# Attention in units of four heads on a fixed clock of twelve matmuls, with engines held to program order

## The chip, the cores and the metric

The kernel runs on one core of one Trainium2 chip. The metric is the device time of one execution, in microseconds (us), as the median of three runs.

## The reference, cut to what matters

One sequence of 256 positions and width 1024 goes through two transformer blocks (the second with weights of its own form), and every product is a float32 product.

```python
def first_block(x, ...):                # DEPTH = 2, layer 0 even, layer 1 odd
    h = x
    for layer in range(DEPTH):
        hn = rmsnorm(h, mix_norm[layer])
        if layer % 2 == 0:
            h = h + moba_nsa_mixer(hn, ...)     # 8 MoBA heads + 8 NSA heads of 64
        else:
            h = h + fox_mixer(hn, ...)          # 16 heads, cumulative forget bias
        h = h + sqrelu_mlp(rmsnorm(h, mlp_norm[layer]), mlp_w1[layer], mlp_w2[layer])
    return rmsnorm(h, final_norm)

def second_block(x, c, ...):
    n = modulate(rmsnorm_2(h, g_ffn1), sh1, sc1);  h = h + 0.5 * gt1 * swiglu(n, ...)
    n = modulate(rmsnorm_2(h, g_mix), sh2, sc2);   h = h + gt2 * hybrid_mixer(n, ...)  # pooling + 8 heads
    n = modulate(rmsnorm_2(h, g_ffn2), sh3, sc3);  h = h + 0.5 * gt3 * swiglu(n, ...)
    return rmsnorm_2(h, g_final)

# in fox_mixer, per head and block of 128 queries:
cum = jnp.cumsum(log_f, axis=1)
s = einsum('bhqd,bhkd->bhqk', qc, k) * scale + cq[..., None] - cum[:, :, None, :]
p = masked_softmax(s, key_pos <= t);   o = einsum('bhqk,bhkd->bhqd', p, v)
```

## The kernel before, in words

**Weight products.** Activations stand transposed, features on partitions and 256 positions along the row. A product with a weight matrix is split in high and low halves (type fp32r) and made of three matmuls per tile (`mm3`, L331 to L333): high by high, high weight by low activation, low weight by high activation. 8304 such matmuls are issued, each 256 (or 258) columns wide. The weights come from HBM in raw tiles of up to 1 MB on SP's DMA queue. Each raw tile is converted in two halves of 128x1024: ACT copies it into a high half (`wh`, L237), DVE subtracts that from the raw tile into the low half (`wl`, L238). Five buffers of each hold the halves, so a half is converted while the four before it are used (`conv`, L219, and `Weights.half`, L251).

**The other work** is put between the weight matmuls. After every twelve weight matmuls the program calls `poke` (L298). It writes one conversion, then the steps of a norm whose countdown is over (`later`, `stage`), then one step of background work (`bg`, L281), where up to two generators are under way.

**Attention** is written as such generators. A `pair_unit` (L645) takes two heads of 64: the scores (QK, L650 and L651, one bank of PSUM per head), on DVE the bias and the row minimum (L660, L661), on ACT the exponentials (L662, L664), on DVE the division (L668 to L676), on PE three transposes per head (L681) with a copy by ACT (L683), and the product with the values (PV, L694 and L696). There are 24 such pairs: eight for NSA (two branches of four), four for MoBA, eight for forget attention (layer 1), four in the hybrid mixer. A third branch of NSA attends to compressed keys (`compress`, `cmp_unit`, L944 to L1053).

**The order of each engine's queue** is not the program's: a scheduler orders the instructions by their dependences and its own estimates. A PSUM bank is taken by tag (`bank(tag, 2)`, L82): four tags, `g`, `a`, `accA` and `accB`, with two banks each.

**Norms.** The squares are summed over the partitions by matmuls (L482), POOL takes the inverse root, and `spread` (L494) brings it to all partitions: ACT writes a diagonal (L497), two float32 matmuls with a matrix of ones broadcast it (L498), ACT copies it out (L500). At a stage's end `feed` (L473) splits the new activations into high (L423, ACT) and low (L424, DVE), which the next stage's first matmuls read.

**Forget attention** needs the running sum of the log gates in every partition. `forget` (L1097): two transposes on PE (L1111), a scan on DVE (L1114), one DMA to DRAM (`cd`, L1116) and four back (`hh<-cd`, 512 KB each, L1118), all issued by ACT, then per four heads one add of the causal mask on POOL (L1122), and per head one more (`pre`, L1149).

## Time and profile before

| | |
|---|---|
| median of 3 runs | 1129.63 us (1129.22 to 1130.44) |
| profiled execution, its own time | 1130.82 us |
| span of its trace | 1128.6 us |
| PE busy | 1107.9 us, 98% |
| DVE busy | 806.9 us, 71% |
| ACT busy | 580.6 us, 51% |
| POOL busy | 95.1 us, 8% |
| DMA moved | 233.72 MB, 207 GB/s on average |

The time outside the span (2.2 us) lies before the first and after the last traced instruction. Matmuls overlap in the records: a weight matmul is listed with 0.28 us, yet the next one starts after less than half of that, so times on PE are read from start to start. A row with "x4" joins four records of one line that follow one another; a float32 matmul leaves two records.

### The profile page before, as it was taken

The page shows a single profiled execution, that of the slowest core. Times are in us where ns is not written, and L with a number is a line of the kernel's source. Part 1 is how long each engine was busy: PE and PEld are TensorE (multiplying, and loading weights), DVE is VectorE, ACT ScalarE, POOL GpSimd, SP SyncE. Part 2 cuts the span into 40 slices and gives each one's busy share as a digit, 9 for nine tenths or more (in the row PEclk, how much of TensorE's full clock was granted, in tenths as well). Part 3 has the DMA queues.
Part 4 walks back from the last instruction along what each step waited for, and adds up shares of the span by engine and source line. Part 5 has one row for each costly group of instructions (what it writes and reads, how often), then busy time and mean ns, then how long its engine had stood idle before and what let it go on. Part 6 is the DMA issues. An engine that isn't in the chain of part 4 may idle for free.

```text
span 1128.6 us, 22520 instructions
## 1 busy us (share of the span) xinstructions
PE 1107.9 (98%) x9104; PEld 1070.4 (95%) x9104; DVE 806.9 (71%) x1547; ACT 580.6 (51%) x975; POOL 95.1 (8%) x135
## 2 busy tenths in 40 slices
PE   8999999999999999999999999999999999999997
PEld 7868899999999999999999999999999999999997
DVE  6657678887876665887878777756587867775654
ACT  5466556454546655654544655544455465444432
POOL 3000020000012400300000320000020010000001
PEclk9899999999999999999999999999999999999999
DMA  8954259999986643689998657565474546656521
GB/s 239 331 188 150 76 165 335 314 322 304 311 256 201 207 142 113 222 284 315 305 305 282 183 157 200 181 183 183 148 220 150 151 113 191 185 184 187 178 85 38
DMA packets 243720, 233.72 MB, mean 207 GB/s; under 512 B 6353, under 2 KB 227185, under 8 KB 243617
## 3 DMA queue, kind: packets, MB, share of 16 engines
q1 hardware_dynamic: 242272, 229.37, 64.8%
q10 hardware_dynamic: 1184, 2.73, 0.7%
q8 instruction: 71, 1.16, 0.4%
q14 instruction: 33, 0.26, 0.1%
q0 software_dynamic: 160, 0.19, 0.1%
HBM read 230.42 MB, written 1.85 MB: 206 GB/s over the span
## 4 chain that ended last, share of the span: by engine, by line
PE 89%; DVE 5%; ACT 3%; issue 1%; DMA 1%; SPq 0%; POOL 0%; POOLq 0%; ACTq 0%
PE g L331 10%; PE g L332 10%; PE g L333 10%; PE accA L332 6%; PE accA L331 6%; PE accA L333 6%; PE a L333 6%; PE a L331 6%; PE a L332 6%; PE accB L332 5%; PE accB L331 5%; PE accB L333 5%; DVE wl L238 2%; DVE nl L424 1%; PE a L651 1%; PE accA L681 1%
## 5 line engine op out<-in xcount | busy, mean ns | idle before, releaser
L238 DVE TENSOR_TENSOR wl<-raw,wh 128x1024 fp32r<-128x1024 f32 (+3 forms) x356 | 427.4, 1205 | 207.2 <-ACT wh L237 206.1
L237 ACT ACTIVATE wh<-raw 128x1024 fp32r<-128x1024 f32 (+3 forms) x356 | 365.8, 1033 | 367.3 <-PE accB L332 101.7
L331 PE MATMUL g<-nh,wh 128*128 128x256 f32 (+1 forms) x880 | 253.3, 288 | 0.3 <-DVE ev L1287 0.3
L332 PE MATMUL g<-nl,wh 128*128 128x256 f32 (+1 forms) x880 | 250.2, 284 | 3.3 <-DVE nl L424 3.3
L333 PE MATMUL g<-nh,wl 128*128 128x256 f32 (+1 forms) x880 | 249.9, 284 | 0.0
L331 PEld LDWEIGHTS g<-nh,wh 128*128 128x128 f32 x880 | 167.6, 190 | 6.7 <-issue 4.7
L332 PEld LDWEIGHTS g<-nl,wh 128*128 128x128 f32 x880 | 167.3, 190 | 5.2 <-DVE nl L424 5.0
L333 PEld LDWEIGHTS g<-nh,wl 128*128 128x128 f32 x880 | 167.3, 190 | 1.3 <-DVE wl L238 0.7
L333 PE MATMUL a<-nh,wl 128*128 128x258 f32 (+1 forms) x576 | 162.8, 283 | 0.0
L331 PE MATMUL a<-nh,wh 128*128 128x258 f32 (+1 forms) x576 | 162.3, 282 | 0.0
L332 PE MATMUL a<-nl,wh 128*128 128x258 f32 (+1 forms) x576 | 162.0, 281 | 0.0
L332 PE MATMUL accB<-hl,wh 128*128 128x256 f32 x432 | 123.1, 285 | 0.0
L332 PE MATMUL accA<-hl,wh 128*128 128x256 f32 x432 | 123.1, 285 | 0.0
L333 PE MATMUL accB<-hh,wl 128*128 128x256 f32 x432 | 120.8, 280 | 0.0
L333 PE MATMUL accA<-hh,wl 128*128 128x256 f32 x432 | 120.7, 279 | 0.0
L331 PE MATMUL accA<-hh,wh 128*128 128x256 f32 x432 | 120.4, 279 | 0.0
L331 PE MATMUL accB<-hh,wh 128*128 128x256 f32 x432 | 120.3, 279 | 0.0
L331 PEld LDWEIGHTS a<-nh,wh 128*128 128x128 f32 x576 | 109.0, 189 | 0.0
L332 PEld LDWEIGHTS a<-nl,wh 128*128 128x128 f32 x576 | 108.9, 189 | 0.0
L333 PEld LDWEIGHTS a<-nh,wl 128*128 128x128 f32 x576 | 108.7, 189 | 0.0
L408 DVE SCALAR_TENSOR_TENSOR ada<-ada,cb 128x1024 f32<-128x1024 f32 x72 | 87.7, 1219 | 16.1 <-DMA ada<-in_w_adaT_dram 15.7
L331 PEld LDWEIGHTS accA<-hh,wh 128*128 128x128 f32 x432 | 81.2, 188 | 0.0
(298 smaller groups left out, 1971.6 us busy)
## 6 DMA issues: line engine op xcount, KB each, us to landing
raw<-in_mlp_w_dram SPq DMA_DIRECT2D x64, 1024.0 KB, 7.2
ada<-in_w_adaT_dram SPq DMA_DIRECT2D x72, 512.0 KB, 5.9
raw<-in_w_gate_dram SPq DMA_DIRECT2D x44, 512.0 KB, 4.0
raw<-in_w_up_dram SPq DMA_DIRECT2D x44, 512.0 KB, 5.3
raw<-in_w_down_dram SPq DMA_DIRECT2D x16, 1024.0 KB, 5.2
raw<-in_odd_w_in_dram SPq DMA_DIRECT2D x11, 1024.0 KB, 5.7
raw<-in_even_w_in_dram SPq DMA_DIRECT2D x8, 1024.0 KB, 7.7
raw<-in_w_in_dram SPq DMA_DIRECT2D x8, 1024.0 KB, 5.7
```

The costliest lines, as they stand in the source:

```text
L237: state["conva"] = act.activation(his[u][:, k:k + m], r[:, k:k + m], AF.Copy).ins
L238: state["conv"] = dve.tensor_tensor(los[u][:, k:k + m], r[:, k:k + m], his[u][:, k:k + m].bitcast(F32), OP.subtract).ins
L331: pe.matmul(ps, wh, xh, start=start, stop=False, **kw)
L332: pe.matmul(ps, wh, xl, start=False, stop=False, **kw)
L333: state["mm"] = pe.matmul(ps, wl, xh, start=False, stop=stop, **kw).ins
L408: dve.scalar_tensor_tensor(t, t, 1.0, cb, op0=OP.mult, op1=OP.mult, accum_out=modT[:, i:i + 1])
L424: dve.scalar_tensor_tensor(l[:, j, :S], Ht[:, j, :], g[:, j:j + 1], h[:, j, :S].bitcast(F32), op0=OP.mult, op1=OP.subtract)
L651: pe.matmul(p[:, P:384], q[s, P:S], kk[:, :], start=True, stop=True)
L681: pe.transpose(p[:, c * P:(c + 1) * P], sbs[e][:, c * P:(c + 1) * P], ident)
```

## The change

- **Units of four heads.** `quad` replaces `pair_unit`: twelve units of two pairs each. It writes the QK of all four heads in one place, the two heads of a pair alternating, and the PV of all four in one place.
- **A clock.** `poke` counts ticks of twelve weight matmuls. A generator yields the number of ticks until its next step, and a new unit starts no sooner than SPACE = 5 ticks after the one before. `quick` units, the last of a stage, take fewer ticks.
- **Program order.** Between `begin()` and `end()` each instruction of PE, ACT, DVE and POOL is made to depend on the one before it on its engine, so that the scheduler keeps the order that the program has. Three stretches are enclosed: the NSA and MoBA mixer, the forget mixer, and the hybrid mixer, each with its output projection.
- **Banks.** The eight PSUM banks are one list; `drop` gives a bank back, `bank` takes the one that has been free longest.
- **Conversions in two steps.** The high half (ACT) is written in one tick, the low half (DVE) in a later one. Near a stage's end `hold` stops both until the last `feed`; `ordered` keeps them behind it.
- **Stage ends.** The last weight tile of an FFN and the second half of an output projection finish their outputs one by one; in the output projections `lagged` writes the low split one output later than the high one.
- **Norms.** `diag` makes a high and a low diagonal, one tick before two fp32r matmuls, 256 wide, against ones (L582) replace the four records of before. The mlp's spread comes eight ticks later, that of forget attention one tick later.
- **Queues.** The DMAs of `cd` and `hh<-cd` go from ACT's queue to POOL's. POOL adds the mask to all sixteen heads before the first `pre`. Some adds of NSA's compress branch move from DVE to POOL.

The diff, cut to its core:

```diff
+    def end():
+        code = nc.cur_bb.bb.instructions
+        start = next(n for n in reversed(range(len(code))) if code[n] is since["last"])
+        engines = [x.engine for x in (pe, act, dve, gp_)]
+        chain = {}
+        for n, i in enumerate(list(code)):
+            if i.engine not in engines:
+                continue
+            if n > start and i.engine in chain:
+                tc.add_manual_dep(i, chain[i.engine].name, ..., reason="order")
+            chain[i.engine] = i
...
+        def high():
+            t = sb([P, 1024], F32R, "wh", WB)
...
+                state["conva"] = act.activation(his[u], r[0], AF.Copy).ins
+        def low():
+            t = sb([P, 1024], F32R, "wl", WB)
...
+                state["conv"] = dve.tensor_tensor(los[u], r[0], his[u].bitcast(F32), OP.subtract).ins
...
-    def poke(n=1):
-        if todo and halves[todo[0][0]][0] in raws:
-            todo.popleft()[1]()
+    def poke():
+        clock["t"] += 1
...
-        bg(n)
+        steps()
+        if not state.get("hold"):
+            if lows and (not todo or todo[0][0] > lows[0][0]):
+                lows.popleft()[1]()
+            if todo and halves[todo[0][0]][0] in raws:
+                todo.popleft()[1]()
...
+    def quad(q, k_of, v_of, bias_of, gate_of, o, last, pre=None, quick=False):
...
+        for j in range(2):
+            for e in range(2):
+                ps[j, e] = bank("s")
+            for b in range(2):
+                for e in range(2):
+                    s = slice(64 * e, 64 * e + 64)
+                    c = slice(P * b, P + S * b)
+                    pe.matmul(ps[j, e][:, c], q[s, j, b * P:(b + 1) * P], k_of(j, e)[:, 0:P + P * b],
+                              start=True, stop=True)
...
+            yield 1 if j == 0 or quick else 2
...
+        scale(0)
+        yield 1
...
+    def spread(dg, dst):
+        ps = bank("r")
+        for i in range(2):
+            pe.matmul(ps[:, :S], ones_r, dg[:, i].rearrange("p b c -> p (b c)"), start=i == 0, stop=i == 1)
...
-        norm_begin(1e-5, 3, 6)
+        begin()
+        norm_begin(1e-5, 4, 7)
...
-            act.dma_start(cd, cs[:, 0])
+            gp_.dma_start(cd, cs[:, 0])
             for x in (3, 2, 1, 0):
-                act.dma_start(cumb[x // 2][:, 4 * (x % 2):4 * (x % 2) + 4],
+                gp_.dma_start(cumb[x // 2][:, 4 * (x % 2):4 * (x % 2) + 4],
                               bass.AP(tensor=cd.tensor, offset=cd.offset + 4 * S * x, ap=[[0, P], [S, 4], [1, S]]))
             for x in (3, 2, 1, 0):
...
-                nc.gpsimd.tensor_tensor(part, part, tri[:, None, :].to_broadcast([P, 4, P]), OP.add)
+                gp_.tensor_tensor(part, part, tri[:, None, :].to_broadcast([P, 4, P]), OP.add)
```

**Where it moves instructions.** On PE, at the first scores of NSA, behind a weight product (`s` and `a` are banks of scores, `ada` and `hl` hold keys and queries). Before:

```order
L333 MATMUL g_422<-nh_116,wl_375 128x256
L650 MATMUL a_481<-ada_178,hl_177 128x128
L651 MATMUL a_481<-ada_178,hl_177 128x256
L650 MATMUL a_484<-ada_178,hl_177 128x128
L651 MATMUL a_484<-ada_178,hl_177 128x256
L650 MATMUL a_525<-ada_178,hl_177 128x128
L651 MATMUL a_525<-ada_178,hl_177 128x256
L650 MATMUL a_528<-ada_178,hl_177 128x128
L651 MATMUL a_528<-ada_178,hl_177 128x256
L681 MATMUL accA_598<-cst_92,sb_488 128x128 x3
```

With the change:

```order
L405 MATMUL g_422<-nh_118,wl_376 128x256
L749 MATMUL s_453<-ada_180,hl_179 128x128
L749 MATMUL s_454<-ada_180,hl_179 128x128
L749 MATMUL s_453<-ada_180,hl_179 128x256
L749 MATMUL s_454<-ada_180,hl_179 128x256
L749 MATMUL s_459<-ada_180,hl_179 128x128
L749 MATMUL s_460<-ada_180,hl_179 128x128
L749 MATMUL s_459<-ada_180,hl_179 128x256
L749 MATMUL s_460<-ada_180,hl_179 128x256
L403 MATMUL g_422<-nh_118,wh_378 128x256
```

Before, the two matmuls of one head (L650, L651) followed one another, then those of the next head. Now the two heads of a pair alternate, four heads stand together, and weight matmuls follow at once; the first transposes come 48 weight matmuls later.

On POOL, at the start of forget attention, behind the inverse root of the norm. Before:

```order
L491 TENSOR_SCALAR nat<-nat 128x2
L492 TENSOR_TENSOR nat<-nat 128x2
L1122 TENSOR_TENSOR hh<-hh,cst 128x4x128
L1149 TENSOR_TENSOR sb<-hh,cst 128x128 x4
L1122 TENSOR_TENSOR hh<-hh,cst 128x4x128
L1149 TENSOR_TENSOR sb<-hh,cst 128x128
L1122 TENSOR_TENSOR hh<-hh,cst 128x4x128 x2
L1149 TENSOR_TENSOR sb<-hh,cst 128x128 x11
```

With the change:

```order
L568 TENSOR_SCALAR nat<-nat 128x2
L569 TENSOR_TENSOR nat<-nat 128x2
L1310 DMA cd<-ev 16x256
L1312 DMA hh<-cd 128x1024 x4
L1316 TENSOR_TENSOR hh<-hh,cst 128x4x128 x4
L1339 TENSOR_TENSOR sb<-hh,cst 128x128 x16
L507 TENSOR_TENSOR ssq<-sq 128x256
```

The five DMAs now stand on POOL, and four adds of the mask stand ahead of the first unit's adds (L1339, which were L1149), where before it was one. On PE the scores of the first unit (L749) stand 24 weight matmuls behind the two transposes that begin the chain (L1304, before L1111), and its first transposes (L783) 48 weight matmuls behind the scores.

On ACT, at the same place (`wh` are high halves of weights, `sb` the scores of a head). Before:

```order
L237 ACTIVATE wh_4251<-raw_3974 128x1024
L1116 DMA cd_4261<-ev_4258 16x256
L237 ACTIVATE wh_4295<-raw_3974 128x1024
L1118 DMA hh_4078<-cd_4261 128x1024 x2
L1118 DMA hh_4077<-cd_4261 128x1024 x2
L237 ACTIVATE wh_4327<-raw_4047 128x1024
L237 ACTIVATE wh_4355<-raw_4047 128x1024
L608 ACTIVATE hl_4373<-g_4314,nat_4076 128x256 x2
L237 ACTIVATE wh_4389<-raw_4115 128x1024
L662 ACT_TABLE_LOAD
L662 ACTIVATE sb_4400,rr_4399<-sb_4400,mn_4402 128x128
L664 ACTIVATE sb_4400,rr_4399<-sb_4400,mn_4402 128x256
```

With the change:

```order
L276 ACTIVATE wh_4232<-raw_3965 128x1024
L276 ACTIVATE wh_4276<-raw_3965 128x1024
L761 ACT_TABLE_LOAD
L761 ACTIVATE sb_4309,rr_4329<-sb_4309,mn_4331 128x128
L763 ACTIVATE sb_4309,rr_4329<-sb_4309,mn_4331 128x256
L761 ACTIVATE sb_4311,rr_4329<-sb_4311,mn_4336 128x128
L763 ACTIVATE sb_4311,rr_4329<-sb_4311,mn_4336 128x256
L276 ACTIVATE wh_4341<-raw_4097 128x1024
L761 ACTIVATE sb_4313,rr_4330<-sb_4313,mn_4355 128x128
L763 ACTIVATE sb_4313,rr_4330<-sb_4313,mn_4355 128x256
L761 ACTIVATE sb_4315,rr_4330<-sb_4315,mn_4360 128x128
L763 ACTIVATE sb_4315,rr_4330<-sb_4315,mn_4360 128x256
```

ACT's five DMAs are gone; the exponentials of two heads stand together, one conversion between them and the next two heads. On DVE, the low half that goes with that conversion stands directly ahead of the division (L769) of the first pair.

## Rows read from the trace of the kernel before

**Rows 1.** Chain that ended last (page), then PE's waits: total us, times, longest us.

```profile
PE 89%; DVE 5%; ACT 3%; issue 1%; DMA 1%; SPq 0%; POOL 0%; POOLq 0%; ACTq 0%
...
PE g L332 <- DVE nl L424: 3.3, 8, 0.8
PE a L650 <- DVE mn L661: 1.6, 3, 0.7
PE accA L681 <- DVE sb L675: 1.2, 1, 1.2
PE a L498 <- ACT sq L497: 1.0, 1, 1.0
```

**Rows 2.** Stretches: length, busy us of PE, PEld, DVE, ACT, POOL; clock, DMA.

```profile
40.00:50.50 10.50, 10.32 (x39) 8.28 (x40) 8.32 (x27) 7.67 (x20) 0.00 (x0) 0.51 1.09 346
180.00:240.00 60.00, 60.00 (x510) 60.00 (x510) 50.12 (x65) 29.17 (x34) 0.00 (x0) 1.00 0.96 316
```

**Rows 3.** Timeline of PE, two QK blocks: start us, us, engine, line, operation.

```profile
106.55 0.28 PE L331 MATMUL g<-wh,nh 128*128 128x256 f32 x1
106.76 0.50 PE L650 MATMUL a<-hl 64*128 64x128 f32 x4
107.62 0.39 PE L332 MATMUL g<-wl,nh 128*128 128x256 f32 x1
107.85 0.28 PE L333 MATMUL g<-wh,nl 128*128 128x256 f32 x1
...
435.57 0.48 PE L650 MATMUL a<-hl 64*128 64x128 f32 x2
436.98 0.39 PE L331 MATMUL accA<-nh,wh 128*128 128x256 f32 x1
```

**Rows 4.** Timeline of PE around a spread of the norm, layer 1's mlp.

```profile
476.81 0.28 PE L331 MATMUL g<-nh,wh 128*128 128x256 f32 x1
477.04 0.78 PE L498 MATMUL accA<-sq,ones 128*128 128x128 f32 x4
477.78 0.28 PE L333 MATMUL g<-nh,wl 128*128 128x256 f32 x1
```

**Rows 5.** Timeline of PE at the boundary into layer 0's mlp.

```profile
162.29 0.28 PE L331 MATMUL g<-nh,wh 128*128 128x256 f32 x1
163.28 0.39 PE L332 MATMUL g<-nl,wh 128*128 128x256 f32 x1 [0.71 <-DVE nl L424]
```

**Rows 6.** Timelines of PE, DVE and POOL at the start of forget attention.

```profile
359.11 0.38 PE L1111 MATMUL a<-cst,ev 128*16 128x128 f32 x2 [0.58 <-DVE ev L1106]
...
360.86 0.67 DVE L1114 TENSOR_TENSOR_SCAN ev<-ev,a 16x256 f32<-16x256 f32 x1
...
367.47 1.28 POOL L1122 TENSOR_TENSOR hh<-hh,cst 128x512 f32<-128x512 f32 x1 [14.49 <-DMA hh<-cd]
```

**Rows 7.** DMA issues: KB each, median us to landing.

```profile
hh<-cd ACTq DMA_DIRECT2D x4, 512.0 KB, 5.6
...
relb<-in_rel_bias_dram POOLq DMA_DIRECT2D x1, 2.0 KB, 3.8
...
cd<-ev ACTq DMA_DIRECT2D x1, 16.0 KB, 1.4
```

**Rows 8.** Timelines of DVE, then ACT, in the first unit of forget attention.

```profile
371.90 0.29 DVE L660 CUSTOM_DVE_ANT_0 sb<-a,sb 128x128 f32<-128x128 f32 x1 [2.06 <-PE a L651]
...
372.46 1.28 DVE L238 TENSOR_TENSOR wl<-raw,wh 128x1024 fp32r<-128x1024 f32 x1
...
376.87 0.17 DVE L668 RECIPROCAL rr<-rr 128x4 f32<-128x4 f32 x1
...
377.82 0.28 DVE L675 TENSOR_SCALAR sb<-sb,rr 128x128 f32<-128x128 f32 x1
...
372.60 0.40 ACT L662 ACTIVATE sb<-sb,mn 128x128 f32<-128x128 f32 x1
...
373.50 1.04 ACT L237 ACTIVATE wh<-raw 128x1024 fp32r<-128x1024 f32 x1
```

More of the change, by code (lines that the diff above doesn't have):

```diff
@@ L24 @@
 RAW = 5
+SPACE = 5
 WARM = 10
@@ L254, in half @@
             u = unit[self.i, h]
-            while todo and todo[0][0] <= u:
-                todo.popleft()[1]()
+            force(u)
             conv(u + WB - 1)
@@ L277, in step, with go, steps @@
             return False
-    WIDTH = 2
-    def bg(n=1):
-        for _ in range(n):
-            while len(running) < WIDTH and background:
-                running.append(background.popleft())
-            if not running:
-                return
-            g = running.pop(0)
-            if step(g):
-                running.append(g)
+    clock = {"t": 0, "quad": -99}
+    quads = deque()
+    def go(g, at=1):
+        running.append([clock["t"] + at, g])
+    def steps():
+        now = clock["t"]
+        if quads and now >= clock["quad"] + SPACE:
+            clock["quad"] = now
+            running.append([now, quads.popleft()])
+        for x in list(running):
+            if x[0] <= now:
+                try:
+                    x[0] = now + (next(x[1]) or 1)
+                except StopIteration:
+                    running.remove(x)
     ada = {"g": None, "n": 0, "on": False}
@@ L319, in f @@
             opened[key] -= 1
-        background.append(f())
+        if at is None:
+            quads.append(f())
+        else:
+            go(f(), at)
     def settle(key):
+        n = 0
         while opened.get(key, 0):
-            bg()
-    def drain():
-        while running or background:
-            bg()
+            clock["t"] += 1
+            steps()
+            n += 1
+        waits.append((key, n))
+    waits = []
+    tc.waits = waits
     def mm3(ps, wh, wl, xh, xl, start, stop, **kw):
@@ L516, in ordered @@
             return g
-        f2 = ordered(f2)
-        later(n1, ordered(f1))
-        later(n2, last)
+        for n, f in steps:
+            later(n, ordered(f))
+        later(steps[-1][0], last)
     def on_norm(f):
@@ L762, in ffn, with part @@
                 if b == 0:
-                    acc[t] = bank("accA" if t < 2 else "accB", 2)
+                    acc[t] = bank("acc")
                 ps = acc[t]
                 end = b == len(bl) - 1
+                def part(jj, ks):
+                    s = slice(jj * P, (jj + 1) * P)
+                    for k in ks:
+                        mm3(ps[:, jj * S:(jj + 1) * S], w.h(k, s), w.l(k, s), hh[:, k, :], hl[:, k, :],
+                            b == 0 and jj == 0 and k == 0, end and k == m - 1, skip_group_check=True)
+                    poke()
+                if end and t == 3:
+                    state["hold"] = hold
+                    ks = [w.half(h) for h in range(2)]
+                    for jj in range(2):
+                        for x in ks:
+                            part(jj, x)
+                        done(2 * t + jj, ps[:, jj * S:(jj + 1) * S])
+                    drop(ps)
+                    continue
                 for h in range(2):
@@ L768, in ffn @@
                     for jj in range(2):
[L769 to L773 removed]
+                        part(jj, ks)
                 if end:
@@ L1051, in body @@
-        q, k, v = qkv()
+                    pe.matmul(p[64 * e:64 * e + 64, j * S:(j + 1) * S], vrep[c][:, 2 * j + e, :], pt, start=j == 0,
+                              stop=True, skip_group_check=True)
+            o = onsa[:, 2 * c:2 * c + 2, :]
+            i = 4 + 2 * c
+            dve.tensor_tensor(o, o, two(p), OP.add)
+            drop(p)
+            act.activation(oh_[:, i:i + 2, :], o, AF.Copy)
+            yield 1
+            dve.tensor_tensor(ol_[:, i:i + 2, :], o, oh_[:, i:i + 2, :].bitcast(F32), OP.subtract)
@@ L1070, in body, with units @@
+        def units():
+            while opened["c"]:
+                yield 1
+            yield from cmp_unit(0, nq[:, 0])
+        opened["n", 1] = opened.get(("n", 1), 0)
         moba(0)
-        settle("n")
-        settle("c")
-        for c in range(2):
-            push("f", cmp_unit(c, nq[:, c]))
         moba(1)
         settle("f")
-        f = feeder(gain["mlp0"])
-        def done(j, ps):
-            if j == 0:
-                f(None)
-            add_h(j, ps)
-            f(j)
-        out_proj("eout", oh_, ol_, 4, done)
+        new_n()
@@ L1085, in body @@
+        out_proj("eout", oh_, ol_, 4, False, lagged(gain["mlp0"], add_h))
+        end()
         with tc.issue_after(state["load"]):
@@ L1320, in v_trans @@
         def v_trans(vt, v, j):
-            p = bank("a", 2)
+            while not space(1):
+                yield 1
+            p = bank("a")
             for b in range(2):
@@ L1371, in last @@
             dve.tensor_scalar(Hg[:, j, :], Ht[:, j, :], gain["out"][:, j:j + 1], None, op0=OP.mult)
-        swiglu(2, lambda: norm_begin(1e-6, N1, N2, "accB"), last)
-        banks = [[bank(("g", "accA")[h], 2) for h in range(2)] for b in range(2)]
+        swiglu(2, lambda: norm_begin(1e-6), last)
+        banks = [[bank("t") for h in range(2)] for b in range(2)]
         def transposes(js, after):
```

723 lines of the change are left out of this document (408 added, 315 removed).

## Prediction

> **What bounds the kernel now.** I read the chain that ended last first. It should be read for who holds it: PE has 89% of it, DVE 5%, ACT 3%, and all queues together about 1% [rows 1]. So a change pays only where PE waits, where its clock is down, or where it spends time on something that can be written shorter. Then I read the busy time of one long stretch of weight products. PE starts 510 of them in 60.00 us, one per 0.118 us, at full clock [rows 2]; nothing in this change touches that rate, and the number of weight matmuls (8304) stays. What is left is everything between them. For that I read the list of PE's waits [rows 1], and the timelines around the places where other work cuts in [rows 3, 4, 5].
>
> PE's waits are small and few: 3.3 us for low halves of a new stage's activations, 1.6 and 1.2 us in the NSA attention, 1.0 us for the diagonal of a norm [rows 1]. One of them has a long shadow. From 40 to 50.5 us PE was busy for 10.32 of 10.50 us at a granted clock of 0.51, so at the 1.2 GHz level of its two (2.4 GHz is the other) for nearly all of it [rows 2]. It follows directly on the stretch in which the attention units kept PE waiting.
>
> **The change part by part.** The sum stands against the profiled execution's own 1130.8 us; the median of the runs is 1.2 us lower.
>
> *Scores.* A pair whose heads alternate takes 0.86 us from its first start to the next weight matmul (106.76 to 107.62); a pair whose heads follow one another takes 1.41 us (435.57 to 436.98) [rows 3]. By the order of PE before, 12 of the 24 pairs alternate wholly, 3 in part, 9 not. All 24 do now. Gain: 9 x 0.55 + 3 x 0.3, so 5.9 us.
>
> *Fewer cuts.* From the last weight matmul into the scores PE needs 0.21 us instead of 0.12, and from the first weight matmul behind them to the next 0.23 instead of 0.12 [rows 3]: 0.2 us per cut. By the order, score and value products cut into the weights at 41 places before and at most 24 now. Gain: 17 x 0.2, 3.4 us.
>
> *Spreads.* Around a spread, 0.97 us pass from one weight matmul (476.81) to the second one behind it (477.78); two weight matmuls account for 0.24 [rows 4]. The remaining 0.73 us become two fp32r matmuls of the weight matmuls' own width and type, 0.24. There are eight spreads: 3.9 us.
>
> *NSA waits and the clock.* The waits of 1.6 and 1.2 us are four [rows 1], and each refill costs 0.16 us more than it shows: at a boundary 0.99 us pass between starts, of which 0.12 is the matmul and 0.71 the listed wait [rows 5]. Units spaced five ticks apart, their transposes 48 weight matmuls behind their scores, have cover for this: 3.4 us. If PE no longer idles there, the low clock goes too: 10.5 us at 0.51 [rows 2], 5.1 us.
>
> *Stage boundaries.* Eight waits for `nl`, 3.3 us, with eight refills of 0.16 [rows 1, 5], 4.6 us. Outputs that end one by one, splits in steps, and conversions held back shorten this. I leave 1.0 us: 3.6 us gained.
>
> *Norm of forget attention.* The 1.0 us for the diagonal [rows 1], with one refill, and 0.58 us ahead of the transposes of the gates [rows 6] go, since each step now comes a tick later: 1.7 us.
>
> These gains sum to 27.0 us.
>
> *The start of forget attention* is the one place where I see a large new wait. Count from the start of the two transposes that feed the scan. Before, the scan ended at 2.4 us (360.86 + 0.67 - 359.11), and POOL's first add began at 8.4 us [rows 6]. Now the DMAs are issued by POOL. The small one took 1.4 us on ACT's queue; the nearest row for POOL's is a 2 KB load with 3.8 us [rows 7]. So the first add comes at 8.4 to 10.8 us; I take the middle, 9.6, since the 3.8 was seen beside the loads at the kernel's start. Then come four adds of 1.28 us [rows 6] where one sufficed, 14.7 us, and the first head's own add, a quarter as wide (an estimate from the same row: 0.4). The rest of the chain, by the order of ACT and DVE: one head's minimum 0.56 (371.90 to 372.46), the exponentials of two heads 2 x 0.90 (372.60 to 373.50), the conversion that now stands between them and the next pair, 1.04 high and 1.28 low, and the division 0.95 (376.87 to 377.82) [rows 8]. That is 5.6 us, and the first transposes are ready at 20.7 us. PE gets there sooner: 0.2 for the two transposes, 24 weight matmuls 2.8, four heads of scores 1.9, 48 weight matmuls 5.7, together 10.6 us. PE waits 10.1 us. Before, transposes came well after; the scheduler filled in weight matmuls, and program order forbids that now. The low end is 6.6 us (first add at 8.4, conversion not in the chain). The high end is 17 us (the large loads, 5.6 us on ACT's queue [rows 7], twice as slow on POOL's).
>
> The Trainium skill has a rule for this path: "DMA: Bandwidth & Descriptors", section "Anatomy of one DMA — SWDGE (gpsimd) path", gives about 2.0 us fixed plus the bytes at 436 GB/s. By that the small DMA would take 2.0 us and a large one 3.2 us (estimates from the page), the first add would come at 7.7 us, and the predicted time would be some 2 us lower; the row's 3.8 us for 2 KB [rows 7] speaks against it.
>
> *The clock behind that wait.* A wait of that length is longer than any here before. What follows the NSA waits is the nearest row: 5.1 us lost [rows 2]. I take 4.5; bounds 0 and 5.1.
>
> *Waits inside the other units.* From the start of the scores a unit's chain takes 0.86 + 0.56 + 1.8 + 1.04 + 1.28 + 0.95 = 6.5 us [rows 3, 8]; PE reaches the transposes after 1.9 + 5.7 = 7.6 us. So the slack is 1.1 us, and the last unit of a stage, with 36 weight matmuls instead of 48, has none. I take 1.0 us in all; bounds 0 and 8 (what the NSA stretch lost before).
>
> *At nothing:* POOL's adds for the compress branch (POOL has nothing else there; uncovered, they would delay one branch), ACT freed of five DMAs (PE did not wait for ACT there), and the banks' list. Weight loads on SP's queue keep their order.
>
> Sum: 27.0 - 10.1 - 4.5 - 1.0 = 11.4 us less, 1119.4 us for the profiled execution, **1118 us** as a median.
>
> **The rivals.**
>
> A. *The chain of forget attention is short, or the clock holds.* For it: DVE and ACT have time there, and the first add came at 8.4 us with the DMAs on a busy queue. Against: four adds now stand in a row. Stall 6.6, no clock loss, no waits in units: 9 us less, about 1109 us.
>
> B. *Slower: program order costs every unit.* ACT and DVE may no longer move a ready exponential ahead of a conversion that waits for PE to free its buffer. The conversion stands between two pairs of heads, so its wait enters the chain of each of the twelve units. The slack is 1.1 us. The change is slower than no change once each unit waits over 1.14 us (1118.2 + 12 x 1.14 reaches 1131.9), so once the chain is 8.7 us instead of 6.5. With 1.5 us each it is 1136 us. For it: DVE and ACT run at one queue each and conversions occupy them half the time. Against: the buffer comes free when PE goes on behind the scores, 1.9 us after their start, while the exponentials end at 3.2.
>
> C. *It does not do what it says:* the alternation gains nothing where four heads share the place, and cuts cost as before. 9.3 us less gain: 1127 us.
>
> **How the numbers follow.** Forecast 0.54, A 0.24, B 0.14, C 0.08. About 0.2% (2.3 us) can be told from no change. B is slower in most of its cases, and C lies close to no change in some: faster 0.83, same 0.05, slower 0.12. The range goes down to 1104 (A, with a few more waits of the NSA stretch gone that I did not count) and up to 1127 (the stall at its high end, 7 us more, and 2 us in units; C). Left out are most of B and the far end of A.
>
> **What would show it.** Right: 24 alternating pairs near 0.8 us; spreads of 0.24 us; no clock near 0.5 between 40 and 50 us; one long wait of PE, near 10 us, at the first transposes of forget attention, released by DVE, with POOL's adds ahead of it, and a low clock behind it. Wrong: no such wait (A), or waits of a us or more at the first transposes of most units (B).

## The result and the profile after

The changed kernel takes **1149.97 us** (median of 4 runs, 1148.53 to 1151.24); before it was 1129.89 us beside it. The ratio is 1.0178, interval 1.016 to 1.0195: slower, by 20 us. The forecast was 1118 us, faster. The range ended at 1127.

The page's chain that ended last and PE's waits (us in total, times, longest) of the changed kernel answer to [rows 1]:

```profile
PE 77%; DVE 9%; ACT 6%; DMA 4%; issue 2%; POOL 1%; SPq 0%; POOLq 0%; ACTq 0%; DVEq 0%
...
PE t L783 <- DVE sb L775: 13.8, 7, 9.6
PE t L783 <- issue: 7.1, 1, 7.1
PE s L749 <- DVE hl L707: 4.8, 2, 3.5
...
PE a L1503 <- DVE sb L1498: 2.8, 3, 1.2
...
PE acc L403 <- DVE H L1449: 2.2, 2, 1.6
PE a L1523 <- DVE ev L1483: 1.7, 3, 0.9
...
PE acc L403 <- DVE H L868: 1.0, 2, 0.5
...
PE g L404 <- DVE nl L956: 0.5, 2, 0.3
```

PE held 89% of the chain, now 77%; DVE went from 5% to 9%, and DMA from 1% to 4%. The waits that the forecast wanted gone are nearly gone: `nl`, 3.3 us before, is 0.5 us. Others stand in their place. The first transposes of units wait for DVE's division 13.8 us in all, 9.6 of them once, and once 7.1 us, where the view names no releaser ("issue"). The residual adds (`H`, L1449 and L868) hold back an output's bank, which happened nowhere before. L1503 and L1523 are steps of the pooling and of the values in the hybrid mixer.

**Where the time went.** Both traces hold the same 8304 weight matmuls. The n-th one starts at some time in each; the difference of the two times tells where a stretch lost. These are worked out from the timelines of PE, after minus before:

| stretch (weight matmuls) | gained or lost there |
|---|---|
| start, NSA and MoBA (0 to 528) | -1.5 us |
| output projection, mlp of layer 0 (to 2352) | +1.4 us |
| forget attention and its projection (to 2976) | +13.5 us |
| mlp of layer 1, first swiglu (to 6264) | +0.3 us |
| hybrid mixer and its projection (to 6672) | +6.8 us |
| the rest | -0.1 us |

**NSA.** Timelines of ACT, DVE and PE in the changed kernel, at the first unit:

```profile
35.70 2.01 ACT L276 ACTIVATE wh<-raw 128x1024 fp32r<-128x1024 f32 x2 [7.91 <-DMA raw<-in_even_w_in_dram]
...
45.30 1.04 ACT L276 ACTIVATE wh<-raw 128x1024 fp32r<-128x1024 f32 x1
55.11 1.06 ACT L276 ACTIVATE wh<-raw 128x1024 fp32r<-128x1024 f32 x1 [8.77 <-DMA raw<-in_even_w_in_dram]
...
36.80 1.23 DVE L282 TENSOR_TENSOR wl<-raw,wh 128x1024 fp32r<-128x1024 f32 x1 [4.14 <-ACT wh L276]
...
39.82 1.22 DVE L282 TENSOR_TENSOR wl<-raw,wh 128x1024 fp32r<-128x1024 f32 x1
40.95 0.28 DVE L759 CUSTOM_DVE_ANT_0 sb<-s,hh 128x128 f32<-128x128 f32 x1
...
46.37 1.23 DVE L282 TENSOR_TENSOR wl<-raw,wh 128x1024 fp32r<-128x1024 f32 x1 [1.98 <-ACT wh L276]
...
34.37 1.58 PE L749 MATMUL s<-ada,hl 64*128 64x128 f32 x16
...
48.90 0.91 PE L783 MATMUL t<-cst,sb 128*128 128x128 f32 x3 [7.10 <-issue]
```

ACT stood 7.91 us for a weight tile that had not landed yet, and only then converted it. (The tile was no later than before: issued at 28 us in both kernels, it landed 7.6 us later, 7.4 before.) DVE's low half had to follow. PE had the scores of four heads from 34.37 us on, but the first minimum (L759) starts at 40.95, behind two low halves, and the division waits for the low half at 46.37, which waits for the high half at 45.30, which stands behind the exponentials of all four heads. PE comes to the transposes after weight matmul 216 and waits until 48.90. In the kernel before, the exponentials of the first heads ran at 37.12 us and the conversions behind them at 40.30. At 46.3 us ACT stands once more, 8.77 us for a tile whose load the change put behind two others; what that wait costs is not shown apart.

The clock follows. Windows of the changed kernel: length, busy us of PE, PEld, DVE, ACT and POOL, then the granted clock, DMA share and GB/s:

```profile
42.00:46.00 4.00, 0.00 (x0) 0.00 (x0) 2.39 (x11) 3.62 (x15) 0.00 (x0) 1.00 1.10 344
...
50.00:54.00 4.00, 4.00 (x23) 3.63 (x23) 0.85 (x4) 0.00 (x0) 0.00 (x0) 0.52 1.09 323
```

PE did nothing from 42 to 46 us; from 50 to 54 us it is busy throughout, at a granted clock of 0.52. So the low clock of [rows 2] did not go; it came later, for a shorter time (from 54 to 58 us the clock is at 1.00).

**Forget attention.** Timelines of PE, DVE and POOL in the changed kernel; [rows 6] and [rows 8] are their counterparts:

```profile
361.52 0.39 PE L1304 MATMUL a<-cst,ev 128*16 128x128 f32 x2 [0.22 <-DVE ev L1298]
...
368.28 2.93 PE L749 MATMUL s<-hl 64*128 64x128 f32 x16 [3.51 <-DVE hl L707]
...
386.76 0.87 PE L783 MATMUL t<-cst,sb 128*128 128x128 f32 x3 [9.64 <-DVE sb L775]
...
363.12 2.35 DVE L282 TENSOR_TENSOR wl<-raw,wh 128x1024 fp32r<-128x1024 f32 x2
...
365.83 0.67 DVE L1307 TENSOR_TENSOR_SCAN ev<-ev,a 16x256 f32<-16x256 f32 x1
...
367.55 0.67 DVE L707 TENSOR_TENSOR hl<-g,rbc 128x512 f32<-128x512 f32 x1
381.81 0.29 DVE L759 CUSTOM_DVE_ANT_0 sb<-s,sb 128x128 f32<-128x128 f32 x1 [13.59 <-POOL sb L1339]
...
366.80 0.62 POOL L1310 DMA_DIRECT2D cd<-ev  x1 [12.96 <-DVE ev L1307]
...
375.04 1.29 POOL L1316 TENSOR_TENSOR hh<-hh,cst 128x512 f32<-128x512 f32 x1 [2.51 <-DMA hh<-cd]
377.58 3.78 POOL L1316 TENSOR_TENSOR hh<-hh,cst 128x512 f32<-128x512 f32 x3 [1.25 <-DMA hh<-cd]
```

Read from 361.52 us, where the chain begins. The scan ends 5.0 us later (365.83 + 0.67), not 2.4: two low halves (363.12) stand ahead of it. The low half and the evacuation of the keys (L707, 367.55) stand behind it, and PE waits 3.51 us for the keys, a wait that I had not seen. The first add starts after 13.5 us, the first minimum after 20.3, the first transposes after 25.2. Their wait, 9.64 us, is what was forecast (10.1).

```profile
368.20:371.50 3.30, 3.22 (x18) 2.40 (x19) 0.02 (x1) 0.00 (x0) 1.09 (x3) 0.53 1.02 325
371.50:377.00 5.50, 5.50 (x48) 5.42 (x46) 0.00 (x0) 0.00 (x0) 2.31 (x3) 1.00 1.03 350
377.00:386.70 9.70, 0.13 (x2) 0.00 (x0) 3.99 (x20) 4.56 (x18) 6.24 (x9) 0.73 0.11 45
386.70:391.80 5.10, 5.04 (x24) 5.05 (x25) 4.09 (x10) 3.48 (x7) 2.08 (x2) 0.50 0.31 85
```

In these windows the clock is down to 0.53 and 0.50 right behind the two waits, and at 1.00 between them. Four heads of scores took 2.86 us there (368.28 to the next weight matmul at 371.14), against 1.51 us for the unit at 34.37 (to 35.88).

### The profile page after: what moved, and what is told of

Read it like the earlier page. It is cut to its first block, busy times and chain, and to the rows that moved or that the text cites. A ratio compares the mean times of both kernels' runs of the same rounds, so it can differ in the third digit from the quotient of the medians.

```text
span 1149.0 us, 22404 instructions
## 1 busy us (share of the span) xinstructions
PE 1095.1 (95%) x9088; PEld 1064.0 (93%) x9088; DVE 805.9 (70%) x1534; ACT 577.1 (50%) x963; POOL 112.2 (10%) x150
## 4 chain that ended last, share of the span: by engine, by line
PE 77%; DVE 9%; ACT 6%; DMA 4%; issue 2%; POOL 1%; SPq 0%; POOLq 0%; ACTq 0%; DVEq 0%
PE g L404 14%; PE g L403 14%; PE g L405 14%; PE acc L404 10%; PE acc L403 10%; PE acc L405 10%; DVE wl L282 3%; ACT wh L276 2%; DMA raw<-in_even_w_in_dram 1%; ACT sb L763 1%; PE s L749 1%; DMA vd<-ev 1%; PE t L783 1%; ACT sb L761 1%; DMA raw<-in_mlp_w_dram 1%
## 5 line engine op out<-in xcount | busy, mean ns | idle before, releaser
L282 DVE TENSOR_TENSOR wl<-raw,wh 128x1024 fp32r<-128x1024 f32 (+2 forms) x352 | 421.9, 1206 | 188.2 <-ACT wh L276 187.7
L276 ACT ACTIVATE wh<-raw 128x1024 fp32r<-128x1024 f32 (+2 forms) x352 | 362.1, 1036 | 308.7 <-PE acc L404 151.8
L405 PE MATMUL g<-nh,wl 128*128 128x258 f32 (+1 forms) x1600 | 453.0, 283 | 6.0 <-DVE wl L282 3.5
L403 PE MATMUL g<-nh,wh 128*128 128x258 f32 (+1 forms) x1600 | 455.8, 285 | 0.0
L404 PE MATMUL g<-nl,wh 128*128 128x258 f32 (+1 forms) x1600 | 452.4, 283 | 0.8 <-DVE nl L956 0.5
L404 PE MATMUL acc<-hl,wh 128*128 128x256 f32 x864 | 246.1, 285 | 0.0
L403 PE MATMUL acc<-hh,wh 128*128 128x256 f32 x864 | 241.1, 279 | 2.7 <-DVE H L1449 2.2
L405 PE MATMUL acc<-hh,wl 128*128 128x256 f32 x864 | 241.5, 279 | 0.0
L403 PEld LDWEIGHTS acc<-hh,wh 128*128 128x128 f32 x864 | 162.4, 188 | 3.4 <-DVE H L1449 2.6
L404 PEld LDWEIGHTS acc<-hl,wh 128*128 128x128 f32 x864 | 162.4, 188 | 0.0
L483 DVE SCALAR_TENSOR_TENSOR ada<-ada,cb 128x1024 f32<-128x1024 f32 x72 | 88.4, 1229 | 14.0 <-DMA ada<-in_w_adaT_dram 13.5
L783 PE MATMUL t<-cst,sb 128*128 128x128 f32 x144 | 26.7, 294 | 21.1 <-DVE sb L775 13.8
```

The source lines that it names most:

```text
L276: state["conva"] = act.activation(his[u], r[0], AF.Copy).ins
L282: state["conv"] = dve.tensor_tensor(los[u], r[0], his[u].bitcast(F32), OP.subtract).ins
L403: pe.matmul(ps, wh, xh, start=start, stop=False, **kw)
L404: pe.matmul(ps, wh, xl, start=False, stop=False, **kw)
L405: state["mm"] = pe.matmul(ps, wl, xh, start=False, stop=stop, **kw).ins
L483: dve.scalar_tensor_tensor(t, t, 1.0, cb, op0=OP.mult, op1=OP.mult, accum_out=modT[:, i:i + 1])
```

## The experiments

Two theories stood. P: **program order** costs; work whose data are ready stands behind work whose data are late. L: the **ticks place the units too early**, whoever orders the queues.

### Which order costs

**e1**: no chain.

```diff
-        engines = [x.engine for x in (pe, act, dve, gp_)]
+        engines = []
```

> The changed kernel (1150 us) with the chain that holds PE, ACT, DVE and POOL to program order taken out; units, ticks, banks and conversions stay. Theory P (program order is what costs: work whose data are ready stands behind work whose data are late): the wait of 3.5 us ahead of the scores of forget attention goes, the 9.6 us at its first transposes and the 7.1 us at those of NSA shrink to a half, the waits of the hybrid mixer (about 6 us) to a third; with less time at the low clock 1125 to 1133 us. Rival L (the places that the ticks give the units are too early for their data, and a scheduler that orders by its own estimates leaves them there): the waits stay, 1145 to 1152 us.

Measured: 1117.66 us, ratio to before 0.9896 (0.988 to 0.9913): faster than before, 32 us faster than the changed kernel, and faster than either theory expected. PE's waits:

```profile
PE t L783 <- DVE sb L775: 8.6, 1, 8.6
PE acc L403 <- DVE H L868: 2.1, 2, 1.1
```

The 7.1 us at NSA's first transposes, the 3.5 us ahead of the scores of forget attention and the waits of the hybrid mixer are gone. One large wait is left, 8.6 us at forget attention. P is right for most of it; for that one place, L.

**e2**: PE alone in order.

```diff
-        engines = [x.engine for x in (pe, act, dve, gp_)]
+        engines = [pe.engine]
```

> As the changed kernel, but only PE is held to program order; ACT, DVE and POOL are ordered by the scheduler. If it is ACT's and DVE's order that costs (conversions waiting for weights ahead of ready exponentials and minima, evacuations ahead of the scan): 1130 to 1140 us, with the 3.5 us ahead of the scores of forget attention and most of the 7.1 us at NSA's first transposes gone. If it is PE's own order (transposes that may not be overtaken by weight matmuls): 1145 to 1152 us, and both waits as before.

Measured: 1131.39 us, ratio 1.0016 (1.0003 to 1.0028). PE's longest wait:

```profile
PE t L783 <- DVE sb L775: 12.1, 1, 12.1
```

So order on ACT, DVE and POOL accounts for 18.6 us, and PE's own for 13.7 over e1. The expectation took it for one or the other; it is both. With PE in order, the wait at forget attention is 12.1 us, longer than with all in order, since PE gets there without the 3.5 us ahead of the scores.

**e3**: ACT, DVE and POOL in order, PE free.

```diff
-        engines = [x.engine for x in (pe, act, dve, gp_)]
+        engines = [act.engine, dve.engine, gp_.engine]
```

> As the changed kernel, but only ACT, DVE and POOL are held to program order; PE is free. The run with PE alone in order took 1131.4 us, 13.7 more than with no order (1117.7) and 18.6 less than with all (1150.0). If the two costs add up, this one takes 1134 to 1138 us. If order on ACT, DVE and POOL costs only because PE cannot step around what it makes late, the scheduler fills PE's waits with weight matmuls: 1118 to 1125 us.

Measured: 1135.46 us, ratio 1.0041 (1.0026 to 1.0055). The costs add up (13.7 and 17.8 us over e1, 32.3 together). PE's waits now stand at weight matmuls, which wait for conversions and for the evacuation of transposes that are late in ACT's order:

```profile
PE g L403 <- ACT wh L276: 7.5, 1, 7.5
PE g L403 <- ACT pt L785: 5.2, 1, 5.2
```

**e11**: all four engines in order, the conversions of weights left out of it.

```diff
+                loose.append(state["conva"])
...
+                loose.append(state["conv"])
...
-            if i.engine not in engines:
+            if i.engine not in engines or any(i is x for x in loose):
                 continue
```

> As the changed kernel, all four engines in program order, except that the conversions of weights (high on ACT, low on DVE) are left out of the chain. If it is the conversions, waiting for weights or for a buffer, that hold back ready exponentials, minima and divisions behind them: nearly all of what order on ACT and DVE costs goes, 1130 to 1136 us, and the 7.1 us wait at NSA's first transposes with it. If it is the attention's own steps that hold each other back: 1145 to 1150 us.

Measured: 1133.43 us, ratio 1.0025 (1.001 to 1.0039): 16.5 us less with the conversions alone, and the wait of 7.1 us at NSA is gone. Two things remain, the wait at forget attention (9.0 of the 10.5 us) and the hybrid mixer:

```profile
PE t L786 <- DVE sb L778: 10.5, 3, 9.0
PE a L1506 <- DVE sb L1501: 3.8, 3, 1.6
...
PE a L1526 <- DVE ev L1486: 1.8, 2, 1.4
```

L1506 and L1526 are L1503 and L1523 of the changed kernel. In the hybrid mixer PE waits 5.6 us for such steps here. In the changed kernel it waits 4.5 us for them and 1.3 for the keys. So it is not the conversions that make order cost there.

By stretch (start of a weight matmul minus that of the same one before, us, at the end of the stretch less at its begin):

| stretch | all in order | all, conversions left out | PE only | ACT, DVE, POOL only | none |
|---|---|---|---|---|---|
| to 528, NSA and MoBA | -1.5 | -8.0 | -7.7 | -2.1 | -11.2 |
| 2352 to 2976, forget attention | +13.5 | +8.1 | +9.3 | +8.4 | +5.2 |
| 6264 to 6672, hybrid mixer | +6.8 | +8.5 | +2.4 | +0.7 | -2.4 |

(The trace of e11 is of an execution of 1136.4 us, 3 above its median.) Order costs 8 to 10 us in each of the three enclosed stretches (first column less last), 27 us together; the rest of the 32 lies in the stretches behind them. In NSA ACT's and DVE's order does nearly all of it; in the other two both do. Leaving out the conversions gives back 6.5 and 5.4 us in the first two and nothing in the hybrid mixer.

### Forget attention

**e4**: as the changed kernel, the first unit later: at seven ticks behind the clock, 72 weight matmuls behind its old place.

```diff
+            if first:
+                clock["quad"] = clock["t"] + 7 - SPACE
             push("o" if c < 2 else "f", quad(
```

> As the changed kernel, but the first unit of forget attention starts seven ticks (84 weight matmuls, 9.9 us) after its keys are written; its scores move from weight matmul 2412 to 2484. Theory L (the unit is placed ahead of its chain): the 3.5 us at the scores go, the 9.6 us at the first transposes fall to 0 to 4, and with the low clock gone the time is 1132 to 1140 us. If the chain of DMAs and adds moves along with the unit (it starts from something that the unit sets off), the wait stays near 9 us and the time above 1145.

Measured: 1144.14 us, ratio 1.0126 (1.0111 to 1.0141): 5.8 us less than the changed kernel.

```profile
PE t L783 <- DVE sb L775: 13.0, 7, 8.9
...
PE s L749 <- DVE hl L707: 1.3, 1, 1.3
```

The wait ahead of the scores fell to 1.3 us, but the one at the transposes stays at 8.9. Neither side's number came. The place moved by 72 weight matmuls (72 x 0.118 = 8.5 us); but PE, no longer held up ahead of the scores, reached it only some 4 us later, and the chain itself ended 3 us later (389.99 against 386.76 us, at the same start within 0.3 us): its DMAs landed later in this run. L alone does not free the place.

**e5**: as the changed kernel, POOL adds the mask to a quarter of the heads first, to the others three ticks later.

```diff
             for x in (3, 2, 1, 0):
+                if x == 2:
+                    yield 3
                 part = cumb[x // 2][:, 4 * (x % 2):4 * (x % 2) + 4, P:S]
```

> As the changed kernel, but POOL adds the mask to one quarter of the heads ahead of the first unit, and to the other three quarters three ticks later. If the three further adds (3.8 us) are on the path, the wait at the first transposes of forget attention falls from 9.6 to about 6 us and the time by 4 to 6 us, 1144 to 1146. If the landing of the last of the four large DMAs is what it waits for, or the conversion between the exponentials, it stays at 1150.

Measured: 1146.44 us, ratio 1.0146 (1.0128 to 1.0165), 3.5 us less; the longest wait at the transposes is 5.9 instead of 9.6 us. POOL's timeline:

```profile
375.53 1.28 POOL L1318 TENSOR_TENSOR hh<-hh,cst 128x512 f32<-128x512 f32 x1 [2.78 <-DMA hh<-cd]
376.78 1.70 POOL L1341 TENSOR_TENSOR sb<-hh,cst 128x128 f32<-128x128 f32 x4
```

The first head's add follows the first quarter at once. The three adds were on the path, as forecast.

**e6**: no order, the unit as in e4, the adds as in e5 (the three diffs above together).

> The kernel without the chain of program order (1117.7 us), the first unit of forget attention seven ticks later, and POOL adding the mask to one quarter of the heads ahead of it. If what is left at the first transposes there (8.6 us) is a unit placed ahead of its data, the wait falls to 0 to 3 us and the low clock behind it goes: 1105 to 1110 us. If the chain of DMAs is itself pushed back by the later unit, as it was with program order, the wait stays at 6 us or more: 1114 to 1118.

Measured: 1112.53 us, ratio 0.9849 (0.9834 to 0.9863). The wait fell from 8.6 to 3.7 us, between the two expectations. The edit did only half of what it says: without order, the scheduler put three of the four adds ahead of the first head's own all the same, which starts 19.0 us behind the start of the chain (15.1 in e5).

**e7**: no order, the adds as in e5, the unit where it was, and the DMAs on ACT's queue.

```diff
-            gp_.dma_start(cd, cs[:, 0])
+            act.dma_start(cd, cs[:, 0])
...
-                gp_.dma_start(cumb[x // 2][:, 4 * (x % 2):4 * (x % 2) + 4],
+                act.dma_start(cumb[x // 2][:, 4 * (x % 2):4 * (x % 2) + 4],
```

> The kernel without the chain of program order, the five DMAs of the running sum back on ACT's queue, the mask added to one quarter of the heads first; the unit stays where it was (its transposes come 28 weight matmuls, 3.3 us, sooner by the scheduler's estimate). If POOL's queue is what made the small DMA slow (1.4 us on ACT's before; 3.1 to 5.2 us on POOL's), the landing is 1.4 to 2 us again and the chain from scan to first add about 6 us instead of 10; wait at the transposes 3 to 7 us, time 1111 to 1116. If the traffic of the weights sets it, the small DMA takes 3 us or more on ACT's queue too, and the time is 1117 to 1121.

Measured: 1114.79 us, ratio 0.9872 (0.9856 to 0.9889), a wait of 4.9 us. DMA issues of e7 (KB each, median us to landing):

```profile
hh<-cd ACTq DMA_DIRECT2D x4, 512.0 KB, 5.3
...
cd<-ev ACTq DMA_DIRECT2D x1, 16.0 KB, 4.6
```

The time lies in the first band, but its reason is refuted: the small DMA took 4.6 us on ACT's queue, 4.7 on POOL's in e1 and e6, 3.1 in the changed kernel. The 1.4 us of [rows 7] is no property of the queue. It fell into a gap of the weight stream. The DMA engines while the small DMA was under way (columns as in [rows 2]; the last two are their busy share and GB/s), in the kernel before:

```profile
361.56:362.99 1.43, 1.43 (x14) 1.43 (x13) 0.00 (x0) 1.05 (x1) 0.00 (x0) 1.00 0.05 12
```

and in e7:

```profile
349.53:354.17 4.64, 4.36 (x40) 3.78 (x40) 1.78 (x2) 1.06 (x1) 0.00 (x0) 1.00 0.78 233
```

In the traces of the other kernels they moved 230 GB/s or more then. The queue does differ for the rest of the chain. The scan ends 2.9 us after the chain's start in e1 and in e7, and the small DMA takes the same time; POOL's first add begins at 13.1 us in e1 (POOL's queue) and at 11.8 in e7 (ACT's). The large DMAs are issued 0.5 us sooner behind the small one there, and land sooner: their median is 5.3 to 5.9 us in four runs on ACT's queue and 5.9 to 8.0 in ten on POOL's. So of the 5.4 us by which the first minimum comes sooner than in e1, 1.3 go with the queue and 4.2 with the adds.

**e10**: as e7, with the unit at nine ticks behind the clock, 96 weight matmuls behind its old place.

```diff
+            if first:
+                clock["quad"] = clock["t"] + 9 - SPACE
```

> No chain of program order, the five DMAs on ACT's queue, the mask added to one quarter of the heads first, and the first unit of forget attention nine ticks later (its first transposes at weight matmul 2556, 168 behind the transposes that begin the chain, so 20 us). The chain took about 18 us where the DMAs stood on ACT's queue, so no wait of more than 1 us is left there: 1105 to 1109 us. If the wait only moves to the second unit, which then starts a tick later: 1110 to 1114 us.

Measured: **1108.53 us**, ratio 0.9807 (0.9782 to 0.9832). No wait at the first transposes is left in PE's list. With 168 weight matmuls between the start of the chain and the first transposes (72 in the changed kernel, 144 in e4 and e6), the chain is covered.

### The gains

**e8**: as e1, with one head's scores behind the other's.

```diff
-            for b in range(2):
-                for e in range(2):
+            for e in range(2):
+                for b in range(2):
```

> The kernel without the chain of program order, but in each unit the scores of one head are written after those of the other instead of alternating. By the rows of the kernel before (0.86 against 1.41 us per pair) 24 pairs cost 0.55 us more each: 13 us, 1129 to 1132 us, less what the wait at forget attention hides. If four heads in one place overlap anyhow, or alternation gains nothing there: 1117 to 1121 us.

Measured: 1118.91 us, ratio 0.9906 (0.9891 to 0.992): 1.3 us more than e1, not 13. Timeline of PE in e8, a unit of forget attention from its first score to the next weight matmul:

```profile
406.55 1.68 PE L749 MATMUL s<-hl 64*128 64x128 f32 x16
408.16 0.39 PE L403 MATMUL g<-wh,nh 128*128 128x256 f32 x1
```

The same unit in e1:

```profile
405.62 1.58 PE L749 MATMUL s<-hl 64*128 64x128 f32 x16
407.13 0.39 PE L403 MATMUL g<-wh,nh 128*128 128x256 f32 x1
```

1.61 against 1.51 us: the heads overlap in either order. So my reading of the kernel before was wrong. Its order never alternated; each pair stood head by head. What differs is which matmul waits. Two of its pairs in forget attention, in the order of PE with their waits:

```
L650 MATMUL a_4393<-hl_4160 128x128
L651 MATMUL a_4393<-hl_4160 128x256
L650 MATMUL a_4396<-hl_4160 128x128
L651 MATMUL a_4396<-hl_4160 128x256
...
L650 MATMUL a_5175<-hl_4917 128x128 [waits DVE_49]
L651 MATMUL a_5175<-hl_4917 128x256
L650 MATMUL a_5178<-hl_4917 128x128 [waits DVE_49]
L651 MATMUL a_5178<-hl_4917 128x256
```

The first pair waits for nothing; it starts at 370.83 us and takes 0.86 us, heads side by side. In the second each head waits for DVE, which frees its bank; it is the one of 1.41 us in [rows 3]. All four pairs there whose second head waits for nothing overlap; of those whose second head waits for DVE, some do, such as the one at 106.76 us in [rows 3]. So what a unit of four heads brings is, most likely, four free banks ahead of its scores; that was not tried by itself, and PE's row at 435.57 us shows no idle time between the heads. The gain is no smaller than forecast: outside NSA, from first score to next weight matmul, 16 pairs took 17.7 us before, and eight units of 1.51 us take 12.1; that is 5.6 us, where 5.9 were forecast for all 24 pairs.

**e9**: as e1, with the spread of a norm in its old form.

```diff
-        dg = sb([P, 2, 2, P], F32R, "sq")
+        dg = sb([P, 2, P], F32, "sq")
...
-        for i in range(2):
-            pe.matmul(ps[:, :S], ones_r, dg[:, i].rearrange("p b c -> p (b c)"), start=i == 0, stop=i == 1)
+        for b in range(2):
+            pe.matmul(ps[:, b * P:(b + 1) * P], ones, dg[:, b, :], start=True, stop=True)
```

> The kernel without the chain of program order, but the spread of a norm as before: float32 diagonals by ACT alone and two float32 matmuls, at the ticks of the change. If the form of the matmuls is what gains, 0.49 us for each of eight spreads: 1121 to 1123 us. If only the earlier diagonal counts: 1117 to 1119 us.

Measured: 1117.78 us, ratio 0.99 (0.9885 to 0.9915), no difference from e1. Timeline of PE around layer 1's mlp's spread, in e9:

```profile
480.39 0.28 PE L405 MATMUL g<-nh,wl 128*128 128x256 f32 x1
480.52 0.61 PE L580 MATMUL r<-sq,ones 128*128 128x128 f32 x4
...
481.08 0.28 PE L404 MATMUL g<-nl,wh 128*128 128x256 f32 x1
```

and in e1:

```profile
480.82 0.28 PE L405 MATMUL g<-nh,wl 128*128 128x256 f32 x1
480.94 0.40 PE L582 MATMUL r<-sq,onesr 128*128 128x256 f32 x2
...
481.30 0.28 PE L404 MATMUL g<-nl,wh 128*128 128x256 f32 x1
```

From the weight matmul ahead to the second behind it, 0.69 us in the old form and 0.48 in the new, against 0.97 in [rows 4]. So the forecast 0.49 came, but 0.28 of it are there without the new form, most likely from the earlier diagonal, and 0.21 come from the form. Eight times 0.21 is 1.7 us, less than e1's runs differ by (4.0 us), and the total shows nothing of it. Part is lost again: PE waits for the new form's two diagonals in the first swiglu (0.91 and 0.82 us from start to start ahead of two of its spreads in e1's trace, 0.61 and none in e9's).

**e12**: as e10, both outputs of an FFN's last weight tile finished together, as before.

```diff
-                    for jj in range(2):
-                        for x in ks:
-                            part(jj, x)
-                        done(2 * t + jj, ps[:, jj * S:(jj + 1) * S])
+                    for x in ks:
+                        for jj in range(2):
+                            part(jj, x)
+                    for jj in range(2):
+                        done(2 * t + jj, ps[:, jj * S:(jj + 1) * S])
```

> The fastest kernel so far (no chain of program order, DMAs on ACT's queue, late first unit of forget attention: 1108.5 us) with the last weight tile of each FFN finished as before: both outputs together, instead of the first output a tick earlier. The forecast gave the stage boundaries 3.6 us, and this is the part of it that the FFNs carry. If finishing one by one gains, the waits for low halves (nl) at the start of the next stage come back, four boundaries of about 1 us each: 1110 to 1113 us. If PE's new waits for the residual add (1.4 us at L1453, 0.4 at L1555) give the gain back, the time stays at 1107.5 to 1109.5.

Measured: **1107.23 us**, ratio 0.9793 (0.9779 to 0.9807), the fastest of all; e10's is 1.3 us more, a difference about the size of what runs differ by. The wait for the add of the FFN (L1453 in e10, 1.4 us) is gone and no wait for `nl` came back, so finishing one output earlier gives nothing in the FFNs. The same form in the output projections (L868, PE's longest wait now, 2.1 us) was not tried.

## Why the prediction was wrong, step by step

- **Waits inside the other units** is the step that failed: "I take 1.0 us in all; bounds 0 and 8". The chain of 6.5 us against PE's 7.6 added up durations from [rows 8] and let each conversion start as soon as the exponentials ahead of it ended. In the trace conversions wait for weights (7.91 us once) and for buffers, and in program order everything behind them waits too. PE's waits at transposes in NSA and MoBA sum to 10.5 us (7.1, 1.6, 0.9 and 0.9), and order cost 9.7 us in that stretch (table by stretch, first column less last). e11 shows that the conversions' places in the order are 16.5 us of the whole.
- **A term that was missing**: order in the hybrid mixer cost 9.1 us, and hardly at the units, whose transposes wait 0.3 us there. PE waits for the pooling, for the values and for the keys, 5.8 us in seven waits. The sum had nothing for the work beside the units that the order encloses. e11 shows that conversions are not the cause there; which of those steps would have to move was not tried.
- **Rival B** named the mechanism of NSA and had 0.14. Its price was spread evenly, 1.5 us on each of twelve units, and its sign was a wait of a us or more at most of them; besides the first unit of forget attention only two had one (7.1 and 1.6 us), and the later units of forget attention hardly wait (0.3 us once). Its argument against, that the buffer comes free in time, looked at the buffer and not at the weights.
- **NSA waits and the clock**, 8.5 us, and much of what else was counted there did not come: the wait of 7.1 us and the clock of 0.52 replaced the old ones. Without order the stretch gained 11.2 us.
- **The start of forget attention**: the wait at the transposes was right (9.6 for 10.1) by luck, as errors offset each other. The chain took 25.2 us for 20.7: 2.6 more because DVE's order put two conversions ahead of the scan, 1.3 in the DMAs, 1.2 because the second add had to wait for its data, 0.6 less in the rest. PE came 5.0 us later than counted (15.6 for 10.6), because it waited 3.5 us for the keys behind the same conversions and then ran at the low clock. **The clock behind that wait** was given 4.5 us; it was at 0.50 until 391.8, for 5.1 us, which is some 2.5 us lost (an estimate from that row). The whole start (2352 to 2520) cost 16.9 us for 14.6. e5 confirms the three adds.
- **POOL's queue**: the term of 1.2 us (9.6 for 8.4) was put down to a slow small DMA on that queue. From the end of the scan to the first add the changed kernel takes 8.5 us, 2.6 more than the kernel before. 1.6 of them are the small DMA, and by e7 these go with the weight stream beside it, not with the queue. The other 1.0 lie in the issue of the DMAs and in the large one's landing, and e1 and e7 show 1.3 us like that between the queues. By the fit of the Trainium skill ("DMA: Bandwidth & Descriptors", section "Anatomy of one DMA — SWDGE (gpsimd) path") the small DMA would have landed after 2.0 us on POOL's queue, an estimate from the page. It landed after 3.1 us in the changed kernel and 2.9 to 4.7 in the others, so these traces do not agree.
- **Weight loads** were said to keep their order. They do not quite: two tiles of the compress branch now stand ahead of one of NSA's, the tile of the wait of 8.77 us. e1 has the same order of loads and gains in NSA, so this alone does not make the kernel slow.
- **Scores**: the gain came, for another reason (e8). **Spreads**: the 0.49 us came, 0.21 by form and 0.28 by time, less waits for the diagonals. **Stage boundaries**: 3.6 us forecast, almost nothing gained. Before, PE waited 4.2 us for `nl` (3.3 and two waits at `accA`); in e10 it waits for no `nl`, but 3.9 us for residual adds.
- The sum of the gains was about right, in part by luck, since its terms were not: with no order, the DMAs on ACT's queue, three adds and forget attention's first unit later, the change takes 1107 to 1108.5 us, 22 to 23 us less than before, where 27.0 were counted.

What stays open: whether the weight stream is what makes the small DMA slow (it landed after 1.4 us in the one run where the stream paused and after 3 to 5 in the others; no edit tested it), what makes the order cost 9 us in the hybrid mixer, and how much of the 13.7 us of PE's own order is the order itself, rather than other places that the scheduler then gives the weight matmuls.

## What to carry to other kernels

Fixing an engine's order is safe only if everything in it is ready when its turn comes; add up when inputs arrive, not only how long steps take, and leave work that waits for loads or buffers (here weight conversions) out of the order. Do this sum for all work that the order encloses, not only for the units that the change is about. A long chain with DMAs in it needs its distance in work of the bounding engine counted from its start (here some 20 us, 168 weight matmuls), and a scheduler's own estimate did not give it. Where an order seems to explain a speed in the trace, look at the waits in it too.

## What the runs showed of the hardware

- The score matmuls of two heads, 64 partitions each, ran side by side even when written one head after the other: 1.61 us for four heads, 1.51 when alternating.
- PE's clock was at the lower of its two levels (1.2 of 2.4 GHz) right behind waits of very different length. After 3.5 us of waiting it was 0.53 for 368.2 to 371.5 us and 1.00 in the next 5.5 us; after 9.6 us it was 0.50 for 386.7 to 391.8.
- A DMA of 16 KB landed after 1.4 us while the DMA engines moved 12 GB/s, and after 2.9 to 4.7 us beside a weight stream of 230 GB/s or more (4.3 to 4.6 on ACT's queue, 2.9 to 4.7 on POOL's).
